# Banded attention on one core: TensorE's order fixed by hand, a tile's scores made beside the preceding tile

## The chip, the core and the metric

The kernel runs on one core of a Trainium2 chip. The metric is the device time of one execution in microseconds (us), lower is better. The engines are TensorE (PE in the rows, its weight loads PEld), VectorE (DVE), ScalarE (ACT), GpSimd (POOL, not used here) and SyncE (SP, which issues the DMAs). Each takes its instructions in the order in which they stand in its own list, and waits for the others by semaphores.

## What is computed

Two blocks of a model, each with two layers. The change lies in the attention of the second block's last layer: 256 tokens and 256 context tokens, 16 query heads that share 4 key and value heads of 64 channels, a window of 128 positions to both sides, and a sink, one more logit for each head that takes a share of the softmax and gives no value. Cut to what matters:

```python
s_ctx = einsum('bqhgd,bkhd->bhgqk', qb, kc)
s_win = where(allowed, einsum('bqhgd,bkhd->bhgqk', qb, kb), -inf)
p = softmax(concat([sink, s_ctx, s_win], -1), -1)[..., 1:]
o = einsum('bhgqk,bkhd->bqhgd', p[..., :ctx_len], vc) + einsum('bhgqk,bkhd->bqhgd', p[..., ctx_len:], vb)
x = x + gate * (o @ w_out)
```

Here only the tokens' outputs are needed, since the layer is the last.

## The kernel before, in words

The kernel is written with Python loops that are unrolled, and a scheduler orders each engine's instructions by priority (the place in the program) and by when it takes their inputs to be ready. Activations lie as channels by positions. `swa` (L1362) projects keys, values and queries, norms and rotates them, and then handles the 16 heads in eight tiles of two heads, `attend(t, ...)` (L1311). The output projection `residual` follows.

A tile t has two blocks of 128 queries (b) and two heads (f). For a block and a head:
- scores `swa_s`: two products of 512 columns, the keys' high and low part against queries of which the two halves of the partitions hold high and low part (L1326), and the band's mask, added by a product with the identity (L1327);
- the row maximum on VectorE (L1328), for both heads then the negative scaled maximum `swa_nm` (L1330) and the sink's logit `swa_es` (L1331);
- the exponential `swa_p` on ScalarE with its sum in `swa_z` (L1334);
- four transposes to `swa_pt` (L1337), copied to `swa_ps` by ScalarE for head 0 (L1341) and by VectorE for head 1 (L1339).

Then for the whole tile the row scale: the sinks' exponentials (L1342), the sum (L1343), its reciprocal (L1344), spread to 128 columns in `swa_zw` (L1346), two transposes into a `swa_pt` bank (L1349) and a copy to `swa_zs` (L1351). The 16 value products `swa_o` (L1357; the trace shows 32, two for each) are multiplied by `swa_zs` (L1360) and split into high and low part `xh`, `xl` for the projection (L139, L140).

Four PSUM banks hold scores (shared with the projections), two hold transposes, one the value products, and one is the chain's own for all other names:

```python
with ch.psum_pool("swas", {"pj": (4, "proj proj2 v swa_s"), "hn": (2, "hn_ss hn_bc swap swa_pt"), "o": (1, "swa_o")}):
```

The second group of queries is normed in `head_group`: sums of squares `hn_ss` (L1255), a chain of small steps on VectorE for the scale, its transposes `hn_bc` (L1264), the rotation product `swap` (L1269) with `swa_u` and `swa_rot` on VectorE, twice. The scheduler was free to lay scores of tiles 0 and 1 between these, and parts of a tile between those of another.

Of the kernel before, what the change touches and what calls it, by code (L numbers as in the profile page):

```python
# [13 lines left out]
AF = mybir.ActivationFunctionType  # L14
ALU = mybir.AluOpType
AX = mybir.AxisListType
PSUM = bass.MemoryType.PSUM

P = 128
D = 1024  # L20
KD = D // P
S = 256
# [80 lines left out]
class Kernel:  # L103
# [1204 lines left out]
            self.mm3(ps, [((x[0][:, k, b // 2, t], x[1][:, k, b // 2, t]), (ws[k // 4][0][:, k % 4], ws[k // 4][1][:, k % 4])) for k in range(KD)])  # L1308
            nc.scalar.activation(out[:, b], ps, AF.Copy)

    def attend(self, t, qs, ks, vs, sink, nsink, y):  # L1311

        nc, ch = self.nc, self.ch
        V, G = nc.vector, nc.scalar
        g = t // 4
        z, nm, es = (ch.loc([P, 2, 2], n, bufs=2) for n in ("swa_z", "swa_nm", "swa_es"))
        ps = ch.loc([P, 2, 4, 2, P], "swa_ps", bufs=2)
        for b in range(2):
            q, own = slice(b * P, (b + 1) * P), slice((1 - b) * P, (2 - b) * P)
            m = ch.loc([P, 2], "swa_m", bufs=3)  # L1320
            ss = []
            for f in range(2):
                s = ch.psum([P, 2, S], "swa_s")
                flat = s.rearrange("p j t -> p (j t)")
                for i, k in enumerate(ks):
                    nc.tensor.matmul(flat, qs[:, f, t, q], k[:, f, g].rearrange("p j t -> p (j t)"), start=i == 0, stop=False)  # L1326
                nc.tensor.matmul(s[:, 1, own], self.identb, self.tri[:, 1 - b], start=False, stop=True)  # L1327
                V.tensor_reduce(m[:, f:f + 1], s, AX.XY, ALU.max)  # L1328
                ss.append(s)
            V.scalar_tensor_tensor(nm[:, b], m, -0.125, nsink, op0=ALU.mult, op1=ALU.min)  # L1330
            V.tensor_tensor(es[:, b], nm[:, b], sink, op=ALU.add)  # L1331
            for f, s in enumerate(ss):
                p = ch.loc([P, 2, S], "swa_p", bufs=4)
                G.activation(p, s, AF.Exp, bias=nm[:, b, f:f + 1], scale=0.125, accum_out=z[:, b, f:f + 1])  # L1334
                pt = ch.psum([P, 4, P], "swa_pt")
                for k in range(4):
                    nc.tensor.transpose(pt[:, k], p[:, k // 2, (k % 2) * P:(k % 2 + 1) * P], self.ident)  # L1337
                if f:
                    V.tensor_copy(ps[:, f, :, b], pt)  # L1339
                else:  # L1340
                    G.activation(ps[:, f, :, b], pt, AF.Copy)  # L1341
        G.activation(es, es, AF.Exp)  # L1342
        V.tensor_tensor(z, z, es, op=ALU.add)  # L1343
        V.reciprocal(z, z)  # L1344
        zw = ch.loc([P, 2, P], "swa_zw", bufs=2)
        G.activation(zw.rearrange("p b (f d) -> p (b f) d", f=2), z.rearrange("p b f -> p (b f)").unsqueeze(2).to_broadcast((P, 4, 64)), AF.Copy)  # L1346
        zb = ch.psum([P, 2, P], "swa_pt")
        for b in range(2):
            nc.tensor.transpose(zb[:, b], zw[:, b], self.ident)  # L1349
        zs = ch.loc([P, S], "swa_zs", bufs=2)  # L1350
        G.activation(zs, zb.rearrange("p b t -> p (b t)"), AF.Copy)  # L1351
        o = ch.psum([P, S], "swa_o")
        for b in range(2):
            for k in range(4):
                for f in range(2):
                    v = vs[:, k, 64 * (2 * g + f):64 * (2 * g + f) + 64]
                    nc.tensor.matmul(o[64 * f:64 * f + 64, b * P:(b + 1) * P], v, ps[:, f, k, b], start=k == 0, stop=k == 3,  # L1357
                                     tile_position=(0, 64 * f))
        on = ch.loc([P, S], "swa_on", bufs=2)
        V.tensor_tensor(on, o, zs, op=ALU.mult)  # L1360
        self.split(on, y[0][:, t], y[1][:, t])

    def swa(self, h, x, gate):

        nc, ch, A = self.nc, self.ch, self.A
        V, G = nc.vector, nc.scalar
        with ch.phase("swa"):
            with ch.psum_pool("swas", {"pj": (4, "proj proj2 v swa_s"), "hn": (2, "hn_ss hn_bc swap swa_pt"), "o": (1, "swa_o")}):
                self.swa_tables = [self.load_const(n, F32, ch.ph) for n in ("swa_cos", "swa_sin")]
                qs = ch.loc([P, 2, 8, S], "swa_q", F32R)  # L1370
                ks = [ch.loc([P, 2, 2, 2, S], n, F32R) for n in ("swa_kh", "swa_kl")]
                vs = ch.loc([P, 4, S], "swa_v")
                one = [t[:, :, 1] for t in x]
                keys = self.project_apart([(A["swa_w"], 8 + i) for i in range(2)], x, lambda: self.kv_values(x, vs, (0, 1)))
                self.head_group([keys[i][:, j] for j in range(2) for i in range(2)], self.col("swa_k_gain"), (False, True),
                                lambda i, t: self.stack_keys(ks, i // 2, t))
                for g in range(2):
                    self.head_group([lambda i=i: self.project(A["swa_w"], 4 * g + i, one) for i in range(4)], self.col("swa_q_gain"),
                                    (True, True), lambda i, t: self.stack_queries(qs, 4 * g + i, t))
                    if g == 0:  # L1380
                        self.kv_values(x, vs, (2, 3))
                y = self.own
                sink = self.col("swa_sink")
                nsink = ch.loc([P, 16], "swa_nsink")
                V.tensor_scalar(nsink, sink, -1.0, None, op0=ALU.mult)
                for t in range(8):
                    self.attend(t, qs, ks, vs, sink[:, 2 * t:2 * t + 2], nsink[:, 2 * t:2 * t + 2], y)
                return self.residual(h, A["swa_out"], y, gate)


# [259 lines left out]
```

## Time and profile before

| | us |
|---|---|
| median of 3 runs (lowest, highest) | 3152.95 (3150.81, 3155.64) |
| the profiled execution, its own time | 3151.34 |
| its span in the trace | 3149.4 |
| TensorE, matmuls busy (weight loads) | 3093.1 (2689.0) |
| VectorE, ScalarE busy | 2284.7, 1747.3 |
| mean granted clock of TensorE, as a share of full speed | 0.993 |

Times within the span count from its start. A timeline row is: start, duration, engine, line, operation, output<-inputs, shapes, count of merged instructions, and in square brackets the idle time of the engine just before, with what ended it. Matmuls overlap in TensorE's pipeline, so a row's duration is longer than the step to the next row; the step is what a matmul costs in a dense stretch.

### The profile page before, as it was taken

What the parts mean: (1) busy time and instruction counts of PE and PEld (TensorE: products, weight loads), DVE (VectorE), ACT (ScalarE), POOL (GpSimd) and SP (SyncE); (2) the same over time, 40 slices, a digit from 0 to 9 for tenths busy, and PEclk for the clock granted to TensorE, in tenths of its full rate; (3) what the DMA queues carried; (4) which work ended last, traced back from release to release, by engine and by line L of the source; (5) the groups of instructions that cost most, each with busy time, mean ns of one, the idle gap of its engine ahead of it and who ended that gap; (6) DMA issues with size and microseconds to landing.
All of it is one profiled execution on the core that took longest, in us unless ns stands there. A gap on an engine that the chain in (4) does not pass through costs nothing.

```text
span 3149.4 us, 54554 instructions
## 1 busy us (share of the span) xinstructions
PE 3093.1 (98%) x20526; PEld 2689.0 (85%) x20526; DVE 2284.7 (73%) x4912; ACT 1747.3 (55%) x3553; POOL 0.2 (0%) x4
## 2 busy tenths in 40 slices
PE   8999999999999989999999999999999999998999
PEld 8978999999889988888777778888888888895899
DVE  7767776877777786566788888767776766676666
ACT  5546555655565554444576767545554455565554
POOL 0000000000000000000000000000000000000000
PEclk9999999999999999999999999999999999999999
DMA  7563556666445544443311111245553444440465
GB/s 243 182 211 127 168 177 212 206 186 191 162 160 182 182 134 128 131 140 122 91 41 35 34 48 35 94 135 165 162 170 111 144 139 141 140 137 21 128 182 166
DMA packets 129720, 437.91 MB, mean 139 GB/s; under 512 B 14513, under 2 KB 18225, under 8 KB 129073
## 3 DMA queue, kind: packets, MB, share of 16 engines
q1 hardware_dynamic: 129456, 434.43, 43.7%
q8 instruction: 161, 2.64, 0.3%
q14 instruction: 103, 0.84, 0.1%
HBM read 432.28 MB, written 1.05 MB: 138 GB/s over the span
## 4 chain that ended last, share of the span: by engine, by line
PE 91%; DVE 4%; ACT 2%; DMA 1%; issue 1%; SPq 0%; ACTq 0%; DVEq 0%
PE gu L165 15%; PE gu L166 15%; PE gu L167 14%; PE dn L165 7%; PE dn L166 7%; PE dn L167 6%; PE proj L166 4%; PE proj L165 4%; PE proj L167 4%; PE ada L476 1%; DVE wlo L140 1%; PE dn_pw L995 1%; PE swa_o L1357 1%; PE dn_px L995 1%; PE ms L220 1%
## 5 line engine op out<-in xcount | busy, mean ns | idle before, releaser
L139 ACT ACTIVATE whi<-raw 128x512 fp32r<-128x512 f32 (+1 forms) x1398 | 841.1, 605 | 1026.0 <-PE gu L166 513.0
L140 DVE TENSOR_TENSOR wlo<-raw,whi 128x512 fp32r<-128x512 f32 (+1 forms) x1398 | 913.6, 658 | 543.0 <-ACT whi L139 524.4
L165 PE MATMUL gu<-xh,whi 128*128 128x256 f32 (+1 forms) x2800 | 907.0, 324 | 11.7 <-ACT xh L306 8.8
L166 PE MATMUL gu<-xl,whi 128*128 128x256 f32 (+1 forms) x2800 | 906.5, 324 | 0.2 <-DVE xl L307 0.2
L167 PE MATMUL gu<-xh,wlo 128*128 128x256 f32 (+1 forms) x2800 | 905.2, 324 | 0.1
L165 PEld LDWEIGHTS gu<-xh,whi 128*128 128x128 f32 x2800 | 529.7, 189 | 63.2 <-ACT xh L306 10.7
L166 PEld LDWEIGHTS gu<-xl,whi 128*128 128x128 f32 x2800 | 529.6, 189 | 52.3 <-issue 5.4
L167 PEld LDWEIGHTS gu<-xh,wlo 128*128 128x128 f32 x2800 | 529.1, 189 | 49.7 <-issue 3.7
L165 PE MATMUL dn<-hh,whi 128*128 128x256 f32 (+1 forms) x1388 | 444.9, 322 | 1.3
L166 PE MATMUL dn<-hl,whi 128*128 128x256 f32 (+1 forms) x1388 | 444.3, 321 | 0.0
L167 PE MATMUL dn<-hh,wlo 128*128 128x256 f32 (+1 forms) x1388 | 443.1, 320 | 0.0
L165 PE MATMUL proj<-xh,whi 128*128 128x256 f32 (+2 forms) x936 | 306.0, 330 | 4.9 <-ACT lora_raw L550 1.9
L166 PE MATMUL proj<-xl,whi 128*128 128x256 f32 (+2 forms) x936 | 307.5, 329 | 2.0 <-DVE xl L299 1.6
L167 PE MATMUL proj<-xh,wlo 128*128 128x256 f32 (+2 forms) x936 | 306.8, 329 | 1.6 <-DVE wlo L140 1.6
L165 PEld LDWEIGHTS dn<-hh,whi 128*128 128x128 f32 x1388 | 260.5, 188 | 27.3 <-ACT hh L139 5.5
L166 PEld LDWEIGHTS dn<-hl,whi 128*128 128x128 f32 x1388 | 260.8, 188 | 24.2 <-DVE hl L140 2.8
L167 PEld LDWEIGHTS dn<-hh,wlo 128*128 128x128 f32 x1388 | 260.3, 188 | 21.1
L436 DVE TENSOR_TENSOR ada_t<-ada_w,ada_c 128x1024 f32<-128x1024 f32 x192 | 226.3, 1219 | 0.0
L437 ACT ACTIVATE ada_t<-ada_t 128x1024 f32<-128x1024 f32 x192 | 201.2, 1050 | 29.9 <-DVE ada_t L436 29.5
L165 PEld LDWEIGHTS proj<-xh,whi 128*128 128x128 f32 (+1 forms) x936 | 176.0, 189 | 16.6 <-issue 5.5
L166 PEld LDWEIGHTS proj<-xl,whi 128*128 128x128 f32 (+1 forms) x936 | 176.8, 189 | 15.0 <-DVE xl L299 4.5
L167 PEld LDWEIGHTS proj<-xh,wlo 128*128 128x128 f32 (+1 forms) x936 | 176.7, 189 | 11.4 <-issue 2.4
(521 smaller groups left out, 3769.6 us busy)
## 6 DMA issues: line engine op xcount, KB each, us to landing
raw<-in_ffn_gate SPq DMA_DIRECT2D x176, 512.0 KB, 3.6
raw<-in_ffn_up SPq DMA_DIRECT2D x176, 512.0 KB, 3.6
ada_w<-in_ada_w SPq DMA_DIRECT2D x96, 512.0 KB, 3.6
raw<-in_ffn_down SPq DMA_DIRECT2D x80, 448.0 KB, 3.4
adaw<-in_ada_w SPq DMA_DIRECT2D x48, 512.0 KB, 4.9
raw<-in_ffn_down SPq DMA_DIRECT2D x40, 512.0 KB, 3.5
raw<-in_ffn_down SPq DMA_DIRECT2D x48, 384.0 KB, 3.2
raw<-in_dn_w SPq DMA_DIRECT2D x32, 512.0 KB, 3.5
```

Of the source, the lines that this page charges most:

```text
L139: self.nc.scalar.activation(hi, src, AF.Copy)
L140: return self.nc.vector.tensor_tensor(lo, src, hi.bitcast(F32), op=ALU.subtract)
L165: self.nc.tensor.matmul(out, ah, bh, start=first and i == 0, stop=False)
L166: self.nc.tensor.matmul(out, ah, bl, start=False, stop=False)
L167: self.nc.tensor.matmul(out, al, bh, start=False, stop=last and i == n - 1)
L220: self.nc.tensor.matmul(ms[:, i, b:b + 1], acc[:, j, b * P:(b + 1) * P], self.ones[:, :1], start=j == 0, stop=j == 1)
L436: V.tensor_tensor(p, w, c[:, s], op=ALU.mult)
L437: G.activation(p, p, AF.Copy, accum_out=sums[:, j, k, s:s + 1])
L476: nc.tensor.matmul(ps[32 * i:32 * i + 32], self.cond[:, k], raw[:, i], start=k == 0, stop=k == KD - 1, tile_position=(0, 32 * i))
L995: nc.tensor.matmul(out[:, c], lhs[:, c], rhs[:, c], start=more is None, stop=True, skip_group_check=more is not None)
L1357: nc.tensor.matmul(o[64 * f:64 * f + 64, b * P:(b + 1) * P], v, ps[:, f, k, b], start=k == 0, stop=k == 3, tile_position=(0, 64 * f))
```

## The change

`attend` now holds the loop over the tiles, and two helpers the parts of a tile: `scores` (scores, maximum, exponentials of one block) and `turn` (transposes and copies of one block). In the loop a tile's first transposes are followed by the next tile's scores of block 0, then its second transposes, the transposes of the row scale, the next tile's scores of block 1, and its value products. Every matmul of these is `pinned`: the scheduler has to place it behind whatever TensorE instruction was written before it. The other engines' instructions, and TensorE's other ones, are ordered by the scheduler as before. `swa_p` has six buffers instead of four, the small tiles three instead of two, and the row scale's transposes `swa_zb` fall to the chain's own bank.

```diff
--- before.py
+++ after.py
@@ -1308,57 +1308,93 @@
             self.mm3(ps, [((x[0][:, k, b // 2, t], x[1][:, k, b // 2, t]), (ws[k // 4][0][:, k % 4], ws[k // 4][1][:, k % 4])) for k in range(KD)])
             nc.scalar.activation(out[:, b], ps, AF.Copy)
-    def attend(self, t, qs, ks, vs, sink, nsink, y):
+    def pinned(self, ins):
+        return self.tc.keep_in_program_order(ins)
+    def scores(self, t, b, qs, ks, sink, nsink, st):
         nc, ch = self.nc, self.ch
         V, G = nc.vector, nc.scalar
         g = t // 4
+        q, own = slice(b * P, (b + 1) * P), slice((1 - b) * P, (2 - b) * P)
+        m = ch.loc([P, 2], "swa_m", bufs=3)
+        ss = []
+        for f in range(2):
+            s = ch.psum([P, 2, S], "swa_s")
+            flat = s.rearrange("p j t -> p (j t)")
+            for i, k in enumerate(ks):
+                self.pinned(nc.tensor.matmul(flat, qs[:, f, t, q], k[:, f, g].rearrange("p j t -> p (j t)"), start=i == 0, stop=False))
+            ss.append(s)
+        for f, s in enumerate(ss):
+            self.pinned(nc.tensor.matmul(s[:, 1, own], self.identb, self.tri[:, 1 - b], start=False, stop=True))
+            V.tensor_reduce(m[:, f:f + 1], s, AX.XY, ALU.max)
+        V.scalar_tensor_tensor(st["nm"][:, b], m, -0.125, nsink, op0=ALU.mult, op1=ALU.min)
+        V.tensor_tensor(st["es"][:, b], st["nm"][:, b], sink, op=ALU.add)
+        for f, s in enumerate(ss):
+            p = ch.loc([P, 2, S], "swa_p", bufs=6)
+            G.activation(p, s, AF.Exp, bias=st["nm"][:, b, f:f + 1], scale=0.125, accum_out=st["z"][:, b, f:f + 1])
+            st["p"].append(p)
+    def turn(self, b, st):
+        nc, ch = self.nc, self.ch
+        for f in range(2):
+            p = st["p"][2 * b + f]
+            pt = ch.psum([P, 4, P], "swa_pt")
+            for k in range(4):
+                self.pinned(nc.tensor.transpose(pt[:, k], p[:, k // 2, (k % 2) * P:(k % 2 + 1) * P], self.ident))
+            if f:
+                nc.vector.tensor_copy(st["ps"][:, f, :, b], pt)
+            else:
+                nc.scalar.activation(st["ps"][:, f, :, b], pt, AF.Copy)
+    def attend(self, qs, ks, vs, sink, nsink, y):
+        nc, ch = self.nc, self.ch
+        V, G = nc.vector, nc.scalar
+        def scores(t, b, st):
+            if t < 8:
+                self.scores(t, b, qs, ks, sink[:, 2 * t:2 * t + 2], nsink[:, 2 * t:2 * t + 2], st)
+        def state(t):
+            st = {n: ch.loc([P, 2, 2], "swa_" + n, bufs=3) for n in ("z", "nm", "es")}
+            return st | {"p": [], "ps": ch.loc([P, 2, 4, 2, P], "swa_ps", bufs=2)}
+        st = state(0)
         for b in range(2):
+            scores(0, b, st)
+        for t in range(8):
+            g = t // 4
+            after = state(t + 1) if t < 7 else None
+            z, es = st["z"], st["es"]
+            self.turn(0, st)
+            scores(t + 1, 0, after)
+            G.activation(es, es, AF.Exp)
+            V.tensor_tensor(z, z, es, op=ALU.add)
+            V.reciprocal(z, z)
+            zw = ch.loc([P, 2, P], "swa_zw", bufs=2)
+            G.activation(zw.rearrange("p b (f d) -> p (b f) d", f=2), z.rearrange("p b f -> p (b f)").unsqueeze(2).to_broadcast((P, 4, 64)), AF.Copy)
+            self.turn(1, st)
+            zb = ch.psum([P, 2, P], "swa_zb")
+            for b in range(2):
+                self.pinned(nc.tensor.transpose(zb[:, b], zw[:, b], self.ident))
+            zs = ch.loc([P, S], "swa_zs", bufs=2)
+            G.activation(zs, zb.rearrange("p b t -> p (b t)"), AF.Copy)
+            scores(t + 1, 1, after)
+            o = ch.psum([P, S], "swa_o")
+            for b in range(2):
                 for k in range(4):
+                    for f in range(2):
+                        v = vs[:, k, 64 * (2 * g + f):64 * (2 * g + f) + 64]
+                        self.pinned(nc.tensor.matmul(o[64 * f:64 * f + 64, b * P:(b + 1) * P], v, st["ps"][:, f, k, b], start=k == 0, stop=k == 3,
+                                                     tile_position=(0, 64 * f)))
+            on = ch.loc([P, S], "swa_on", bufs=2)
+            V.tensor_tensor(on, o, zs, op=ALU.mult)
+            self.split(on, y[0][:, t], y[1][:, t])
+            st = after
     def swa(self, h, x, gate):
@@ -1383,8 +1419,7 @@
                 sink = self.col("swa_sink")
                 nsink = ch.loc([P, 16], "swa_nsink")
                 V.tensor_scalar(nsink, sink, -1.0, None, op0=ALU.mult)
-                for t in range(8):
-                    self.attend(t, qs, ks, vs, sink[:, 2 * t:2 * t + 2], nsink[:, 2 * t:2 * t + 2], y)
+                self.attend(qs, ks, vs, sink, nsink, y)
                 return self.residual(h, A["swa_out"], y, gate)
```

TensorE, tile 6 of the kernel before, from its first transposes on, with scores (`swa_s`) of tile 7 in between; the row scale is the transpose of `swa_zw`:

```order
L1337 MATMUL swa_pt<-ident,swa_p 128x128 x4
L1326 MATMUL swa_s<-swa_kh,swa_q 128x512
L1337 MATMUL swa_pt<-ident,swa_p 128x128 x4
L1357 MATMUL swa_o<-swa_ps,swa_v 64x128
L1326 MATMUL swa_s<-swa_kl,swa_q 128x512
L1327 LDWEIGHTS identb
...
L1337 MATMUL swa_pt<-ident,swa_p 128x128 x4
L1357 MATMUL swa_o<-swa_ps,swa_v 64x128 x3
L1349 MATMUL swa_pt<-ident,swa_zw 128x128 x2
L1357 MATMUL swa_o<-swa_ps,swa_v 64x128 x10
L1326 MATMUL swa_s<-swa_kl,swa_q 128x512
```

The same place now, tiles 1 to 6:

```order
L1346 MATMUL swa_pt<-ident,swa_p 128x128 x8
L1327 MATMUL swa_s<-swa_kh,swa_q 128x512
L1327 MATMUL swa_s<-swa_kl,swa_q 128x512
...
L1330 MATMUL swa_s<-tri,identb 128x128
L1346 MATMUL swa_pt<-ident,swa_p 128x128 x8
L1383 MATMUL swa_zb<-ident,swa_zw 128x128 x2
L1327 MATMUL swa_s<-swa_kh,swa_q 128x512
...
L1330 MATMUL swa_s<-tri,identb 128x128
L1392 MATMUL swa_o<-swa_ps,swa_v 64x128 x16
```

The value products, in four pieces before, are one piece at the end, and the transposes of the row scale now stand ahead of the second block's scores and of all value products.

ScalarE, one tile of the kernel before (tiles 2 to 6), from its first exponentials to its row scale and its split:

```order
L1334 ACTIVATE swa_p,swa_z<-swa_s,swa_nm 128x512 x2
L1341 ACTIVATE swa_ps<-swa_pt 128x4x128
L1334 ACTIVATE swa_p,swa_z<-swa_s,swa_nm 128x512 x2
L1342 ACTIVATE swa_es<-swa_es 128x4
L1341 ACTIVATE swa_ps<-swa_pt 128x4x128
L1346 ACTIVATE swa_zw<-swa_z 128x256
L1351 ACTIVATE swa_zs<-swa_pt 128x256
L139 ACTIVATE xh<-swa_on 128x256
```

ScalarE now, tiles 1 to 6; the exponentials are the next tile's:

```order
L1350 ACTIVATE swa_ps<-swa_pt 128x4x128
L1375 ACTIVATE swa_es<-swa_es 128x4
L1350 ACTIVATE swa_ps<-swa_pt 128x4x128
L1336 ACTIVATE swa_p,swa_z<-swa_s,swa_nm 128x512 x2
L1379 ACTIVATE swa_zw<-swa_z 128x256
L1385 ACTIVATE swa_zs<-swa_zb 128x256
L1336 ACTIVATE swa_p,swa_z<-swa_s,swa_nm 128x512 x2
L139 ACTIVATE xh<-swa_on 128x256
```

The row scale `swa_zw` of a tile stood ahead of all exponentials of the next; it now stands behind those of the next tile's first block. In tile 0 alone it is still ahead of them.

VectorE now, tiles 1 to 6:

```order
L1348 COPY swa_ps<-swa_pt 128x4x128
L140 TENSOR_TENSOR xl<-swa_on,xh 128x256
L1331 TENSOR_REDUCE swa_m<-swa_s 128x1 x2
L1376 TENSOR_TENSOR swa_z<-swa_z,swa_es 128x4
L1348 COPY swa_ps<-swa_pt 128x4x128
L1332 SCALAR_TENSOR_TENSOR swa_nm<-swa_m,swa_nsink 128x2
L1377 RECIPROCAL swa_z<-swa_z 128x4
L1333 TENSOR_TENSOR swa_es<-swa_nm,small 128x2
```

The maximum `swa_nm` of the next tile's first block, and behind it this tile's reciprocal, stand behind the copy of this tile's second transposes.

## Rows read from the trace of the kernel before

**Rows 1.** The page, part 4: shares of the chain that ended last, by engine.
```profile
PE 91%; DVE 4%; ACT 2%; DMA 1%; issue 1%; SPq 0%; ACTq 0%; DVEq 0%
```

**Rows 2.** Busy time by stretch: stretch, length, busy us of PE, PEld, DVE, ACT, POOL; clock; DMA; GB/s.
```profile
2880.00:2890.00 10.00, 9.17 (x76) 6.08 (x76) 6.12 (x15) 5.53 (x16) 0.00 (x0) 1.00 0.00 0
```

**Rows 3.** Timeline of TensorE, first instruction of tiles 0, 1, 2, 7 and behind: start us, us.
```profile
2859.47 0.66 PE L1337 MATMUL swa_pt<-ident,swa_p 128*128 128x128 f32 x4 [1.70 <-DVE swa_u L1272]
...
2868.84 1.09 PE L1337 MATMUL swa_pt<-ident,swa_p 128*128 128x128 f32 x8
...
2876.40 0.66 PE L1337 MATMUL swa_pt<-ident,swa_p 128*128 128x128 f32 x4 [0.81 <-ACT swa_p L1334]
...
2919.68 0.65 PE L1337 MATMUL swa_pt<-ident,swa_p 128*128 128x128 f32 x4 [0.82 <-ACT swa_p L1334]
...
2925.64 0.39 PE L165 MATMUL proj<-xh,whi 128*128 128x256 f32 x1
```

**Rows 4.** Timeline of TensorE in tile 1, which it ran without a break.
```profile
2869.77 0.22 PE L1327 MATMUL swa_s<-tri,identb 128*128 128x128 bf16 x1
...
2871.62 0.38 PE L1349 MATMUL swa_pt<-ident,swa_zw 128*128 128x128 f32 x2
2871.93 1.96 PE L1357 MATMUL swa_o<-swa_ps,swa_v 128*64 128x128 f32 x30
2873.82 0.50 PE L1326 MATMUL swa_s<-swa_kl,swa_q 128*128 128x512 f32 x1
...
2874.21 0.48 PE L1326 MATMUL swa_s<-swa_kh,swa_q 128*128 128x512 f32 x1
...
2875.36 0.23 PE L1327 MATMUL swa_s<-tri,identb 128*128 128x128 bf16 x1
```

**Rows 5.** Timeline of VectorE in tile 6 and at the start of tile 7's scores.
```profile
2910.06 0.69 DVE L1328 TENSOR_REDUCE swa_m<-swa_s 128x1 f32<-128x512 f32 x1
...
2910.73 0.69 DVE L1328 TENSOR_REDUCE swa_m<-swa_s 128x1 f32<-128x512 f32 x1
2911.45 0.16 DVE L1330 SCALAR_TENSOR_TENSOR swa_nm<-swa_m,swa_nsink 128x2 f32<-128x2 f32 x1
...
2912.38 0.69 DVE L1339 COPY swa_ps<-swa_pt 128x512 f32<-128x512 f32 x1 [0.57 <-PE swa_pt L1337]
2913.34 0.69 DVE L1328 TENSOR_REDUCE swa_m<-swa_s 128x1 f32<-128x512 f32 x1 [0.26 <-PE swa_s L1327]
2913.95 0.15 DVE L1343 TENSOR_TENSOR swa_z<-swa_z,swa_es 128x4 f32<-128x4 f32 x1
```

**Rows 6.** Timeline of ScalarE in tile 6.
```profile
2910.18 0.69 ACT L1334 ACTIVATE swa_p<-swa_s,swa_nm 128x512 f32<-128x512 f32 x1 [0.67 <-DVE swa_nm L1330]
...
2910.86 0.68 ACT L1334 ACTIVATE swa_p<-swa_s,swa_nm 128x512 f32<-128x512 f32 x1
...
2914.56 0.41 ACT L1346 ACTIVATE swa_zw<-swa_z 128x256 f32<-128x256 f32 x1
```

**Rows 7.** Timeline of TensorE: three lulls, in square brackets, with what ended them.
```profile
231.00 0.38 PE L165 MATMUL proj<-xh,whi 128*128 128x256 f32 x1 [1.91 <-ACT lora_raw L550]
...
275.59 0.61 PE L683 MATMUL g_t<-ident,g_rows 64*128 64x64 f32 x2 [1.50 <-DVE g_rows L671]
...
2848.97 0.50 PE L1326 MATMUL swa_s<-swa_kh,swa_q 128*128 128x512 f32 x1 [2.75 <-ACT swa_p L1334]
```

**Rows 8.** Busy time by stretch, columns as in rows 2: stretches behind lulls, then tiles 2 to 6.
```profile
232.00:236.00 4.00, 4.00 (x24) 4.00 (x22) 1.24 (x6) 1.01 (x2) 0.00 (x0) 0.57 0.95 352
276.00:280.00 4.00, 3.98 (x14) 2.61 (x15) 3.22 (x8) 1.90 (x6) 0.00 (x0) 0.57 0.34 99
2850.00:2854.00 4.00, 4.00 (x13) 2.25 (x12) 2.24 (x6) 1.96 (x6) 0.00 (x0) 0.57 0.02 4
2860.00:2868.00 8.00, 7.31 (x40) 4.95 (x40) 3.58 (x6) 5.09 (x12) 0.00 (x0) 0.57 0.00 0
2876.00:2920.00 44.00, 39.45 (x313) 26.53 (x314) 27.87 (x73) 26.63 (x73) 0.00 (x0) 1.00 0.01 1
```

More of the change, by code (lines that the diff above doesn't have):

```diff
@@ L1315, in attend @@
         g = t // 4
-        z, nm, es = (ch.loc([P, 2, 2], n, bufs=2) for n in ("swa_z", "swa_nm", "swa_es"))
-        ps = ch.loc([P, 2, 4, 2, P], "swa_ps", bufs=2)
-        for b in range(2):
[L1319 to L1335, printed above, removed]
-                for k in range(4):
[L1337 to L1361, printed above, removed]
+        q, own = slice(b * P, (b + 1) * P), slice((1 - b) * P, (2 - b) * P)
```

## Prediction, made before the changed kernel ran

> **What bounds the kernel now.** I read the chain that ended last first: TensorE holds 91% of it [rows 1], so a change to TensorE's order counts where TensorE waits. Next, the busy time by stretch: in 10 us of the banded attention TensorE shows 9.17 us busy, its weight loads 6.08, VectorE 6.12, ScalarE 5.53, DMA nothing, clock 1.00 [rows 2]. So the stage is about 66 us of 3150, and no engine is full in it. Then the timeline, to cut it into tiles at the first transpose of each: tile 0 begins at 2859.47, tile 1 at 2868.84, tile 2 at 2876.40, tile 7 at 2919.68, and its last value products hand over to the output projection at 2925.64 [rows 3]. Tiles 2 to 6 take (2919.68 - 2876.40) / 5 = 8.66 us each; tile 1 takes 7.56, tile 0 9.37. Each tile begins with a lull of about 0.82 us, for the exponential [rows 3].
>
> **What TensorE needs in a tile.** From tile 1, which ran without a break [rows 3, 4]: 8 transposes, a block's share, in 0.93 us (2868.84 to 2869.77), so 0.94 for a block with a little for the step between groups and 1.88 for a tile; the two row-scale transposes 0.31 (2871.62 to 2871.93); 30 value products 1.89 (to 2873.82), so 2.0 for 32, and 2.2 with the handover between 64- and 128-column tiles. Two sets of scores, with their masks, take 2874.21 to 2875.36 plus the last mask: 1.2; with the masks together I take 1.15 for a block, 2.3 for a tile. Sum 6.7 us, against 8.66 now: this is what a better order could win.
>
> **The change, part by part.**
> Instructions and their forms stay the same in number; no DMA is added or moved, and the stage moves next to no data [rows 2]. The larger rings (six exponentials, three of the small tiles, a bank of its own for the row scale) only take waits away, and I cost them at nothing: the waits that decide below are for data.
>
> What decides is where ScalarE puts the row scale `swa_zw` (L1379 of the change). In tiles 1 to 6 it stands behind the two exponentials of the next tile's first block; these wait for the row maximum `swa_nm`, which on VectorE stands behind two reductions and the second transposes' copy. TensorE's fixed order puts the row-scale transposes ahead of the second block's scores and the 32 value products, so all of these wait for `swa_zw`. Before, they did not: `swa_zw` came before the next tile's exponentials, and TensorE had value products on both sides of its transposes. From the end of the first block's scores to the row-scale transposes, link by link:
> - two reductions: 0.69 each, 0.60 to 0.67 apart [rows 5]: 1.3;
> - the sum `swa_z` (0.07 of VectorE's time, my estimate from how closely its small steps follow in rows 5) and the copy, 0.69 [rows 5]: 0.75;
> - the maximum: 0.16 [rows 5], and 0.04 to ScalarE: 0.2;
> - two exponentials, 2910.18 to 2911.54 [rows 6]: 1.36;
> - `swa_zw`, 0.41 [rows 6], and 0.05 to TensorE: 0.46.
> Together 4.05 us. Of this TensorE fills 0.94 with the second block's transposes, so it stands still for 3.1 us. From there it runs: row-scale transposes 0.3, scores 1.15, values 2.2, first transposes of the next tile 0.94, their scores 1.15: 5.75. A tile takes 4.05 + 5.75 = 9.8 us. Six such tiles take 58.8; tiles 1 to 6 took 2919.68 - 2868.84 = 50.84. **Plus 8.0 us.** If my links are 0.2 wrong, this is 1.2 either way.
>
> Then the clock. After lulls of 1.91, 1.50 and 2.75 us [rows 7] the granted clock fell from 1.00 to 0.50, that is from 2.4 to 1.2 GHz, with means of 0.57 over the 4 us that hold each fall [rows 8]. There are nine falls between 200 and 3140 us (the first two, the seventh and the eighth stand in rows 8), and each lull of 1.5 us or more is followed by one; the lulls of 0.82 of tiles 2 to 6 left it at 1.00 [rows 8]. Six of the nine cost (1 - 0.57) x 4 = 1.7 us of full-speed work each, three cost twice that, in the row from 2860 8 us at a mean of 0.57 [rows 8]. A lull of 3.1 us in each of six tiles, with 6 us of dense work behind it that is all on the path, should therefore cost one short fall per tile: 6 x 1.7 = **plus 10.2 us.** The bounds are nothing (no fall) and 6 x 3.4 = 20.4. I take the short fall, since the long ones in rows 8 had further lulls inside, and here work follows without a break. The Trainium skill ("TensorE: Matmul & The Clock Gate", HAM oscillation) describes the same price, paid anew in each pass of a loop with a wait in it, but only for waits longer than the 3.1 us here; by its rule there would be no fall, and the sum would be +7.6 (rival 2). The rows speak against it: 1.50 us was enough [rows 7].
>
> The start. The first pinned score comes behind the last rotation product (`swap`) of the queries, while before the scores of tiles 0 and 1 filled gaps of the second query group. Cover lost: a block's scores, two reductions, the maximum and the exponentials of tile 0 now come behind the queries, 1.15 + 1.3 + 0.2 + 1.36 = 4.0 us. Gained: up to eight reductions leave VectorE's chain for the queries, 8 x 0.60 = 4.8 [rows 5]; the first transpose at 2859.47 waited for that chain (`swa_u`), not for its own data [rows 3]. So -0.8 if all is gained, +2.4 if a third is; I take +0.8, the middle. Tile 0 keeps a good order (its row scale stands ahead of the exponentials): 6.7 of work and about 1 of waits, 7.7 us at full clock or 9.4 with one fall, against 9.37; I take -0.8. The end: in tile 7, 5.96 us long now [rows 3], there are no next scores, and eight projection products instead of six fit in; I take -0.4, between -1 and 0.
>
> **Sum:** 8.0 + 10.2 + 0.8 - 0.8 - 0.4 = +17.8 us. The profiled execution took 3151.34 us for a span of 3149.4, so it would become 3169.1; it lies 1.6 below the median of the runs, 3152.95, from which I get 3170.8, rounded to **3171**. Less than 0.2%, 6.3 us, can't be told from no change here.
>
> **Rivals.**
> 1. Faster: ScalarE gets the row scale out in time. If `swa_zw` were done within the 0.94 us of the second transposes, TensorE would never stand still and a tile would cost its 6.7 us of work: 6 x (8.47 - 6.7) = 10.6 less, 3142 us. For it: tile 0 has that order, and weight loads of 6.08 in 10 us leave room [rows 2]. The Trainium skill ("Perfetto Trace Analysis", Identifying the Most-Contended Engine) holds that matmul busy time is no good measure of how near TensorE is to its limit, and the weight loads' share a better one; by that the room is there, and the 6.7 of 8.66 us from rows 4 agree. Against it: the printed order of ScalarE in tiles 1 to 6. The point that decides is whether the row scale stands ahead of the exponentials.
> 2. The lulls come, the clock holds: 8.0 - 0.4 = +7.6, 3160.5 us. For it: the lulls are regular, and with long dense work between them. Against: each of [rows 7].
> 3. The falls are long ones, or come with a second lull: +28, 3181 us. For it: three of nine were so, among them this very stage at 2860 [rows 8].
> 4. Nothing to see: the links overlap more than I let them (for instance the first reduction starts under the second block's mask), the start gains its 0.8 us and no lull tips the clock: within 6 us.
>
> **How the numbers follow.** My forecast 0.60, rival 1 0.04, rival 2 0.18, rival 3 0.12, rival 4 0.06. The range takes in rival 2 with its 1.2 and the start's bounds, down to 3157, and rival 3 up to 3184; it leaves out rival 1, most of rival 4 and the worst of rival 3, under 0.2. Slower by over 0.2%: the forecast, rival 3 and nearly all of rival 2, 0.88. Faster: rival 1, 0.04. The rest is 0.08.
>
> **What would show it.** In the profile of the changed kernel: the row-scale transposes at L1383 with an idle of some 3 us before them, six times, released by ScalarE's `swa_zw` at L1379 (right), or none (rival 1). ScalarE's second pair of exponentials waiting about 2 us for `swa_nm`. First transposes 11 to 12 us apart (9.8 in rival 2, 13 in rival 3). Granted clock of 0.50 once in each tile for 3 to 4 us behind the lull. The first score at about 2853 and the first transpose near 2860. The forecast is wrong at its root if tiles 1 to 6 take 8.7 us or less, or if the lull ends at something other than `swa_zw`.

## The result and the profile after

The changed kernel took 3169.62 us (median of 6 runs, 3167.57 to 3174.66), the kernel before 3151.99 (6 runs, 3149.70 to 3155.64). The ratio is 1.0057, with a 95% interval of 1.0044 to 1.0069: slower. Beside two later experiments it was run again, 3165.67 against 3152.57, a ratio of 1.0041 (1.0029 to 1.0053). The profiled execution took 3169.32 us for a span of 3167.4.

The shares of the chain that ended last hardly moved against [rows 1]:

```profile
PE 92%; DVE 4%; ACT 2%; DMA 1%; issue 1%; SPq 0%; ACTq 0%; DVEq 0%
```

They can't show it: 18 us of 3150 are half a per cent. The stage must be cut out. Busy time by stretch of the changed kernel (PE, PEld, DVE, ACT and POOL busy, then the granted clock): the ten us that answer to [rows 2], then tiles 1 to 6, from the first transposes of tile 1 to those of tile 7, then two falls of the clock in them.

```profile
2880.00:2890.00 10.00, 7.31 (x60) 5.76 (x58) 5.26 (x14) 4.79 (x14) 0.00 (x0) 0.83 0.01 2
2873.36:2939.66 66.30, 48.52 (x375) 38.52 (x373) 31.54 (x84) 31.29 (x87) 0.00 (x0) 0.82 0.00 1
2880.00:2884.00 4.00, 4.00 (x36) 3.23 (x36) 1.61 (x4) 1.41 (x4) 0.00 (x0) 0.57 0.00 0
2910.90:2917.60 6.70, 5.82 (x39) 4.91 (x40) 1.61 (x4) 2.66 (x8) 0.00 (x0) 0.50 0.00 0
```

TensorE, busy 9.17 of 10 us before, is busy 7.31. Tiles 1 to 6 take 66.30 us, 11.05 each, where they took 50.84 [rows 3], and their mean clock is 0.82 where it was 1.00. There are six falls in them, one beginning within 0.9 us of each lull's end: five short ones like the row from 2880 and one of twice the length (2910.9 to 2917.6).

The waits of TensorE and of ScalarE in tiles 1 to 6 (engine, tile and line, released by what; us in total, times, longest):

```profile
PE swa_zb L1383 <- ACT swa_zw L1379: 17.8, 6, 3.0
...
ACT swa_p L1336 <- DVE swa_nm L1332: 23.8, 13, 3.0
```

TensorE waits for one thing only, the row scale, six times 2.96 us. One of these waits in the timeline: TensorE in tile 1 and at the start of tile 2, then VectorE and ScalarE in the same tile (start, duration, what, and in square brackets the idle time before it and what ended it).

```profile
2873.36 1.09 PE L1346 MATMUL swa_pt<-ident,swa_p 128*128 128x128 f32 x8
...
2875.34 1.05 PE L1346 MATMUL swa_pt<-ident,swa_p 128*128 128x128 f32 x8
2879.35 0.44 PE L1383 MATMUL swa_zb<-ident,swa_zw 128*128 128x128 f32 x2 [2.96 <-ACT swa_zw L1379]
...
2881.22 3.12 PE L1392 MATMUL swa_o<-swa_ps,swa_v 128*64 128x128 f32 x32
```

```profile
2875.49 1.29 DVE L1331 TENSOR_REDUCE swa_m<-swa_s 128x1 f32<-128x512 f32 x2
2876.69 0.15 DVE L1376 TENSOR_TENSOR swa_z<-swa_z,swa_es 128x4 f32<-128x4 f32 x1
2876.76 0.68 DVE L1348 COPY swa_ps<-swa_pt 128x512 f32<-128x512 f32 x1
2877.36 0.15 DVE L1332 SCALAR_TENSOR_TENSOR swa_nm<-swa_m,swa_nsink 128x2 f32<-128x2 f32 x1
2877.43 0.17 DVE L1377 RECIPROCAL swa_z<-swa_z 128x4 f32<-128x4 f32 x1
```

```profile
2877.55 0.69 ACT L1336 ACTIVATE swa_p<-swa_s,swa_nm 128x512 f32<-128x512 f32 x1 [0.96 <-DVE swa_nm L1332]
...
2878.23 0.68 ACT L1336 ACTIVATE swa_p<-swa_s,swa_nm 128x512 f32<-128x512 f32 x1
...
2878.89 0.41 ACT L1379 ACTIVATE swa_zw<-swa_z 128x256 f32<-128x256 f32 x1
...
2882.80 0.69 ACT L1336 ACTIVATE swa_p<-swa_s,swa_nm 128x512 f32<-128x512 f32 x1 [2.59 <-DVE swa_nm L1332]
```

This is the chain of the prediction, link behind link: two reductions, the sum and the copy, the maximum, two exponentials, and only then `swa_zw`, although the reciprocal that it spreads was ready at 2877.60, 1.3 us before. From 2875.49 to 2879.35 it takes 3.86 us; TensorE has 0.9 us of transposes in it and then stands still for 2.96. Behind the lull the clock falls, and the 32 value products, 1.97 us at full clock (a row of the next run), take 3.12.

The start, answering to the first row of [rows 3] and the third of [rows 7]:

```profile
2853.01 1.12 PE L1264 MATMUL hn_bc<-ident,hn_wide 128*128 128x128 f32 x4 [3.50 <-ACT hn_wide L1259]
...
2865.39 0.66 PE L1346 MATMUL swa_pt<-ident,swa_p 128*128 128x128 f32 x4 [4.03 <-ACT swa_p L1336]
```

Before, the scores of tile 0 were made early, with a lull of 2.75 us ahead of them [rows 7]; now there is a lull of 3.50 us for the queries and one of 4.03 us for the first exponentials.

In this execution the work upstream of the stage, the same in both programs, already ran 4.5 us late (2848.89 against 2844.35 at the last sum of squares of the queries), through falls of the clock that come at other places in each execution; such drift is part of the spread of the runs. So the experiments below are read by tiles 1 to 6 first, and by the ratio second.

### The profile page after: what moved, and what is told of

Read it like the earlier page. It is cut to its first block, busy times and chain, and to the rows that moved or that the text cites. A ratio compares the mean times of both kernels' runs of the same rounds, so it can differ in the third digit from the quotient of the medians.

```text
span 3167.4 us, 54544 instructions
## 1 busy us (share of the span) xinstructions
PE 3093.7 (98%) x20526; PEld 2695.9 (85%) x20526; DVE 2282.6 (72%) x4912; ACT 1746.0 (55%) x3553; POOL 0.2 (0%) x4
## 4 chain that ended last, share of the span: by engine, by line
PE 92%; DVE 4%; ACT 2%; DMA 1%; issue 1%; SPq 0%; ACTq 0%; DVEq 0%
PE gu L165 14%; PE gu L166 14%; PE gu L167 14%; PE dn L165 7%; PE dn L166 7%; PE dn L167 7%; PE proj L166 4%; PE proj L165 4%; PE proj L167 4%; PE ada L476 1%; DVE wlo L140 1%; PE dn_pw L995 1%; PE dn_px L995 1%; PE swa_o L1392 1%; PE dn_pt L995 1%
```

## The experiments

Theory: (a) TensorE waits because ScalarE does `swa_zw` behind the next tile's exponentials while the fixed order has TensorE wait for it; (b) the lull and the clock are two costs, about 8 and 10 us in the prediction's sum. Rivals: any fixed order costs this; the restructured program does; the falls have another cause. Each run was compared with the kernel before, run beside it.

### The row scale first

```diff
-            self.turn(0, st)
-            scores(t + 1, 0, after)
             G.activation(es, es, AF.Exp)
             V.tensor_tensor(z, z, es, op=ALU.add)
             V.reciprocal(z, z)
...
+            self.turn(0, st)
+            scores(t + 1, 0, after)
             self.turn(1, st)
```

> The four small steps of the row scale (the sink's exponential, the sum, the reciprocal, swa_zw) stand ahead of the first transposes and of the next tile's first scores, so that ScalarE does swa_zw before the next tile's exponentials; TensorE's fixed order is the changed kernel's. Theory (the place of swa_zw on ScalarE makes the lull, and the lull makes the clock fall): swa_zw now waits only for the second transposes' copy, 0.47 + 0.69 + 0.41 us against 0.94 us of transposes, so a lull of at most 0.9 us is left; no fall of the clock in tiles 1 to 6; tiles of 6.8 to 7.8 us instead of 11.05, so 20 to 26 us under the changed kernel and 4 to 10 us under the kernel before, a ratio of 0.997 to 0.999. Rival A (any order fixed by hand costs this, wherever the row scale stands): still 10 us or more a tile, within 5 us of the changed kernel. Rival B (the lull goes, but the clock falls for another reason): tiles of 8.5 to 9.5 us, 0 to +5 us against before.

3141.53 us, a ratio of 0.9965 (0.9954 to 0.9977). Tiles 1 to 6 by stretch, two rows of TensorE and two of ScalarE in tile 2:

```profile
2879.19:2920.65 41.46, 38.13 (x374) 30.70 (x373) 31.32 (x84) 29.76 (x85) 0.00 (x0) 1.00 0.01 1
```
```profile
2889.68 0.44 PE L1383 MATMUL swa_zb<-ident,swa_zw 128*128 128x128 f32 x2 [0.55 <-ACT swa_zw L1377]
...
2891.10 1.97 PE L1392 MATMUL swa_o<-swa_ps,swa_v 128*64 128x128 f32 x32
```
```profile
2889.22 0.41 ACT L1377 ACTIVATE swa_zw<-swa_z 128x256 f32<-128x256 f32 x1
...
2890.44 0.68 ACT L1336 ACTIVATE swa_p<-swa_s,swa_nm 128x512 f32<-128x512 f32 x1
```

TensorE's order is the changed kernel's, word for word; ScalarE now does `swa_zw` ahead of the next tile's exponentials. The lull is 0.55 us, the clock 1.00, a tile 6.91 us. That refutes rival A, and shows (a): the loss hangs on whether the row scale's four small steps, `swa_zw` last of them, stand ahead of the next tile's exponentials. The gain is a little larger than the forecast, 0.997 to 0.999.

### The lull filled

```diff
             zb = ch.psum([P, 2, P], "swa_zb")
+            for i in range(22 if 0 < t < 7 else 0):
+                self.pinned(nc.tensor.transpose(zb[:, i % 2], self.ident, self.ident))
```

> The changed kernel with 22 transposes of the identity added in each of tiles 1 to 6 where TensorE stands still for swa_zw, 22 x 0.117 = 2.6 us at full clock; they write into the row scale's bank, which its own two transposes then overwrite. The wait itself stays, TensorE is busy in it. Theory (lull and clock are two costs, and the clock falls because TensorE stands still): no fall in tiles 1 to 6; tiles of 9.3 to 9.8 us; 8 to 11 us under the changed kernel, 6 to 10 us above the kernel before, a ratio of 1.002 to 1.003. Rival A (the falls come from somewhere else, or cost nothing because the path runs on ScalarE and VectorE): tiles stay at 11 us, within 3 us of the changed kernel. Rival B (the filler delays the row scale's transposes): tiles over 11 us, slower than the changed kernel.

3157.11 us, a ratio of 1.0011 (1.0000 to 1.0021). Tiles 1 to 6, and one of the six waits that are left, behind the filler:

```profile
2866.30:2922.24 55.94, 52.55 (x507) 45.13 (x505) 31.56 (x84) 30.44 (x85) 0.00 (x0) 1.00 0.00 1
```
```profile
2869.18 2.56 PE L1383 MATMUL swa_zb<-ident 128*128 128x128 f32 x22
2872.31 0.44 PE L1385 MATMUL swa_zb<-ident,swa_zw 128*128 128x128 f32 x2 [0.57 <-ACT swa_zw L1379]
```

From the second transposes to the row scale's it is 4.01 us (2868.30 to 2872.31), as in the changed kernel (2875.34 to 2879.35): the wait is untouched. Only the clock is, 1.00 where it was 0.82. 132 transposes that nobody needs made the stage 66.30 - 55.94 = 10.36 us faster. So the two costs part: the stall is 55.94 - 50.84 = 5.10 us, the clock 10.36. The ratio came out under the 1.002 to 1.003 of the forecast, since the stall is smaller than the 8 us of the prediction's sum.

### The lull half filled

As above, with `range(11 if ...)`.

> As the filler run, but with 11 added transposes instead of 22: 1.3 us of the 2.96 us are filled, a lull of about 1.9 us is left in each of tiles 1 to 6, and the row scale's transposes start no earlier or later. Theory (a lull of this length is answered by a fall of the clock, as the one of 1.91 us early in the profile of before was; what the filler saved was the clock and not the wait): the falls are back in tiles 1 to 6, tiles of about 11 us, within 4 us of the changed kernel, a ratio of 1.004 to 1.007. Rival A (only the full lull of 3 us matters to the clock): no falls in tiles 1 to 6, tiles of 9.3 us, and the ratio of the full filler, 1.000 to 1.002. Rival B: falls in some tiles, and a time between the two.

3157.25 us, a ratio of 1.0017 (1.0009 to 1.0026).

```profile
2872.89:2928.83 55.94, 45.35 (x440) 37.93 (x439) 31.57 (x84) 30.39 (x85) 0.00 (x0) 1.00 0.00 1
```
```profile
PE swa_zb L1385 <- ACT swa_zw L1379: 10.6, 6, 1.8
```

My theory missed here, and rival A was right: six lulls of 1.77 us, and no fall. The tiles take 55.94 us to the hundredth, as with the full filler, which bears out the split into 5.10 and 10.36. But it takes away a reason that the prediction gave for the clock's term, as told below.

### The row-scale transposes last

```diff
-            zb = ch.psum([P, 2, P], "swa_zb")
-            for b in range(2):
-                self.pinned(nc.tensor.transpose(zb[:, b], zw[:, b], self.ident))
-            zs = ch.loc([P, S], "swa_zs", bufs=2)
-            G.activation(zs, zb.rearrange("p b t -> p (b t)"), AF.Copy)
             scores(t + 1, 1, after)
             o = ch.psum([P, S], "swa_o")
...
+            zb = ch.psum([P, 2, P], "swa_zb")
+            for b in range(2):
+                self.pinned(nc.tensor.transpose(zb[:, b], zw[:, b], self.ident))
+            zs = ch.loc([P, S], "swa_zs", bufs=2)
+            G.activation(zs, zb.rearrange("p b t -> p (b t)"), AF.Copy)
             on = ch.loc([P, S], "swa_on", bufs=2)
```

> Only the place of the two row-scale transposes in TensorE's fixed order changes: behind the value products instead of ahead of the second block's scores. Theory (TensorE loses the time because its queue waits at these transposes with ready work behind them): swa_zw may come 3 us later without anybody waiting, so no lull over 1 us and no fall in tiles 1 to 6; tiles of 6.8 to 7.8 us; 20 to 26 us under the changed kernel, 4 to 10 us under the kernel before, a ratio of 0.997 to 0.999. Rival A (the chain of reductions, maximum and exponentials bounds a tile whatever stands where): a wait of 2 to 3 us turns up at another place, the first transposes of a tile, and tiles stay over 9.5 us.

3141.36 us, a ratio of 0.9960 (0.9946 to 0.9974).

```profile
2878.32:2917.73 39.41, 37.69 (x379) 31.34 (x377) 30.10 (x84) 29.85 (x85) 0.00 (x0) 1.00 0.00 1
```
```profile
PE swa_zb L1391 <- ACT swa_zw L1379: 1.7, 5, 0.4
```

Here `swa_zw` is still behind the exponentials of the next tile's first block, but TensorE asks for it 3 us later, with the second block's scores and the 32 value products done in between. A tile takes 6.57 us, less than the 6.8 to 7.8 of the forecast. Either end of the wait can be moved: earlier on ScalarE or later on TensorE. What costs is a fixed place ahead of ready work.

### Without the fixed order

```diff
     def pinned(self, ins):
 
-        return self.tc.keep_in_program_order(ins)
+        return ins
```

> The changed kernel's program, but TensorE's instructions aren't held to the program's order: the scheduler places them, as before, and puts the row-scale transposes of a tile behind its value products. Theory (only where the fixed order puts the row-scale transposes matters): no lull over 1.5 us in tiles 1 to 6, tiles of 7 to 8.5 us, and the first scores fill gaps of the queries again, so the start's 1 to 2 us come back; 16 to 26 us under the changed kernel, between 9 us under and 2 us above the kernel before. Rival (the restructured program, its larger rings and the row scale's own bank, costs the time): over 9.5 us a tile, within 6 us of the changed kernel.

3137.07 us, a ratio of 0.9950 (0.9937 to 0.9963). From the row-scale transposes of tile 1 to those of tile 7 TensorE has no idle time, 38.05 us or 6.3 a tile; below it, two rows of tile 5:

```profile
2870.35:2908.40 38.05, 38.05 (x391) 32.21 (x389) 30.32 (x82) 29.64 (x83) 0.00 (x0) 1.00 0.01 2
```
```profile
2891.81 0.44 PE L1346 MATMUL swa_pt<-ident,swa_p 128*128 128x128 f32 x2
2892.08 0.38 PE L1383 MATMUL swa_zb<-ident,swa_zw 128*128 128x128 f32 x2
```

In tiles 3 to 6 the scheduler puts the row scale's transposes between the next tile's first ones, where by then nobody has to wait for `swa_zw`. A tile was forecast at 7 to 8.5 us, too long. The restructured program without the fixed order is faster than before by 0.5%, so the restructuring doesn't cost the time. Which part of it wins (the order of the program, the larger rings, the bank of its own) was not tried.

### The start, and the best order

Three runs on one chip, the changed kernel again among them, and later a fourth. In one, only the scores of tile 0 were left out of the fixed order; in another, moreover, the row-scale transposes stand behind the next tile's first transposes; the fourth run has this second edit alone.

```diff
-    def pinned(self, ins):
+    def pinned(self, ins, t=1):
 
+        if t == 0:
+            return ins
         return self.tc.keep_in_program_order(ins)
...
-                self.pinned(nc.tensor.matmul(flat, qs[:, f, t, q], k[:, f, g].rearrange("p j t -> p (j t)"), start=i == 0, stop=False))
+                self.pinned(nc.tensor.matmul(flat, qs[:, f, t, q], k[:, f, g].rearrange("p j t -> p (j t)"), start=i == 0, stop=False), t)
...
-            self.pinned(nc.tensor.matmul(s[:, 1, own], self.identb, self.tri[:, 1 - b], start=False, stop=True))
+            self.pinned(nc.tensor.matmul(s[:, 1, own], self.identb, self.tri[:, 1 - b], start=False, stop=True), t)
```
```diff
+        self.turn(0, st)
         for t in range(8):
...
-            self.turn(0, st)
             scores(t + 1, 0, after)
...
-            zb = ch.psum([P, 2, P], "swa_zb")
-            for b in range(2):
-                self.pinned(nc.tensor.transpose(zb[:, b], zw[:, b], self.ident))
-            zs = ch.loc([P, S], "swa_zs", bufs=2)
-            G.activation(zs, zb.rearrange("p b t -> p (b t)"), AF.Copy)
             scores(t + 1, 1, after)
...
+            st = after
+            if t < 7:
+                self.turn(0, st)
+            zb = ch.psum([P, 2, P], "swa_zb")
+            for b in range(2):
+                self.pinned(nc.tensor.transpose(zb[:, b], zw[:, b], self.ident))
+            zs = ch.loc([P, S], "swa_zs", bufs=2)
+            G.activation(zs, zb.rearrange("p b t -> p (b t)"), AF.Copy)
             on = ch.loc([P, S], "swa_on", bufs=2)
```

> The changed kernel with the scores of tile 0 alone not held to the program's order; tiles 1 to 7 as they were. Theory of the prediction (the pinned start loses 4.0 us of cover and gains about 3 us on VectorE's chain for the queries): the 4.0 us lull ahead of the first transposes goes, the queries end later, and 0 to 3 us are won over the changed kernel; tiles 1 to 6 stay at 11 us. Rival A (the whole cover of 4.0 us and a fall of the clock are lost by the pinned start): 4 to 7 us won. Rival B (VectorE's chain decides): nothing won, or up to 2 us lost.

> The changed kernel as it is, beside the two others on the same chip: 1.004 to 1.007 of the kernel before, by every theory; it shows how far the runs of one kernel differ from one set to the next.

> Fixed order again, with two edits: the row-scale transposes of a tile behind the first transposes of the next tile, so that swa_zw has 0.9 us more than where they stood behind the value products (there 0.34 us of wait was left in each tile), and the scores of tile 0 not held to the program's order, so that the scheduler can put them among the queries again. Theory (TensorE's work alone is left, 6.2 us a tile, and the start comes back as in the kernel without fixed order): tiles of 6.1 to 6.4 us, no lull over 0.5 us in tiles 1 to 6, no lull of 3 to 4 us ahead of the first transposes; 3132 to 3139 us, a ratio of 0.9935 to 0.996, level with the kernel without fixed order or up to 5 us under it. Rival (a fixed order is worse than the scheduler's even with the waits out of it): above that kernel by 2 us or more.

> The run with both edits, without the freed scores of tile 0: fixed order throughout, the row-scale transposes behind the next tile's first transposes. Theory (the start is worth nothing either way, and the 0.34 us of wait that the place behind the value products left is gone): tiles of 6.2 us against 6.55 there, so 3137 to 3141 us, within 3 us of the run with both edits. Rival (the freed scores of tile 0 harm, because the clock stayed at half for 17 us at the start of that run): 3 to 6 us faster than it, 3132 to 3135 us.

Ratios: tile 0's scores free 1.0035 (1.0023 to 1.0047), the changed kernel beside it 1.0041 (1.0029 to 1.0053), both edits 0.9949 (0.9938 to 0.9961), the second edit alone 0.9968 (0.9955 to 0.9981). By stretch: tiles 1 to 6 of the changed kernel again; the start of the run with tile 0's scores free; tiles 1 to 6 with the second edit alone.

```profile
2873.84:2941.66 67.82, 50.01 (x375) 39.73 (x373) 31.58 (x84) 32.02 (x88) 0.00 (x0) 0.80 0.00 1
```
```profile
2848.60:2865.90 17.30, 12.95 (x40) 8.13 (x40) 10.48 (x22) 7.75 (x18) 0.00 (x0) 0.52 0.01 1
```
```profile
2870.79:2907.95 37.16, 37.16 (x374) 30.74 (x372) 29.75 (x82) 29.25 (x84) 0.00 (x0) 1.00 0.01 2
```

The freed start wins nothing that can be told: the two ratios' intervals overlap almost wholly. From the last of the queries' sums of squares to the first transposes of tile 1 it takes 24.07 us (2844.13 to 2868.20) against 24.45 (2849.39 to 2873.84): the lull of 4.0 us goes, but the one ahead of the queries' `hn_bc` grows from 3.50 to 4.38 us (below), and in this execution the clock stays at half for 17 us, where there were two short falls.

```profile
2850.36 0.90 PE L1264 MATMUL hn_bc<-ident,hn_wide 128*128 128x128 f32 x3 [4.38 <-ACT hn_wide L1259]
```

The second edit leaves TensorE without a pause in tiles 1 to 6: 37.16 us, 6.19 a tile (37.32 in the run with both edits, 6.22), as forecast in both. That is the work alone. With both edits the time is level with the scheduler's order, as forecast; with the second alone it is 3140.47 us, within the forecast's 3137 to 3141, so its rival, that the freed start harms, falls. But against the run with the transposes last, its gain of 0.38 us a tile, 2.2 us in all, doesn't show in the ratios (0.9968 and 0.9960): that is below what these runs can tell.

## Why the prediction was right, and where its sizes were off

The time was: 3171 predicted, 3169.62 measured, well inside the range. By steps, in the profiled execution:

- **The mechanism: right.** The row-scale transposes wait for `swa_zw` six times, 2.96 us where 3.1 was predicted; ScalarE's second exponentials wait for `swa_nm`, 2.59 us in tile 1 (about 2 predicted); first transposes 11.05 us apart (11 to 12 predicted).
- **The stall: +5.1 us instead of +8.0.** This is the term most mis-sized. With the lull filled, a tile is 9.32 us and not 9.8. From the first transposes to the second it takes 2.00 us (2866.30 to 2868.30), 2.09 predicted; from the second to the row scale's 4.01 (4.05 predicted, though the links listed there add up to 4.07); from there to the next tile's first transposes 3.32 (2872.31 to 2875.63), and here the prediction had 3.65. Its parts: row-scale transposes 0.19 us (0.3 predicted), a block's scores 1.23 (1.15), the 32 value products 1.90 (2.2, of which 0.2 for a handover between tiles of 64 and 128 columns that no run shows). Six times 0.48 are the 2.9 us.
- **The clock: +10.4 instead of +10.2**, from 66.30 - 55.94, which is closer than its reasons deserve: by the prediction's own prices, five short falls and a long one would have been 11.9; in the second profile of the changed kernel, with two long falls instead of one, 67.82 - 55.94 = 11.9. But the reason was wrong in part: the prediction held that each lull of 1.5 us or more is followed by a fall, from [rows 7, 8]. Six lulls of 1.77 us were not. The lulls here were nearly 3 us, so the term stood. The Trainium skill ("TensorE: Matmul & The Clock Gate", HAM oscillation) warns only of idle gaps longer than any of these six; by its rule there would have been no fall. The trace disagrees: the six lulls of 2.96 us each brought one, and so did one of 2.32 us in the run with tile 0's scores free.
- **The start and tile 0: 0 together, as predicted**, with larger parts: 24.47 us from the last sum of squares of the queries to tile 1 (2848.89 to 2873.36), 24.49 before (2844.35 to 2868.84). Tile 0 itself takes 7.97 us instead of 9.37 (-1.4, predicted -0.8), although a fall lies in it, for which the prediction had 9.4; the start took the rest (+1.4, predicted +0.8). Freeing tile 0's scores won no more than 0.4 us of it.
- **The end: -0.7** (tile 7 takes 5.26 us, 2939.66 to 2944.92, for 5.96), -0.4 predicted.

The stage is thus 5.1 + 10.4 + 0 - 0.7 = 14.8 us longer where the prediction had 17.8. The medians say 17.6 in one set of runs and 13.1 in the other; that the forecast came within 1.4 us of the first is partly luck. The profiled execution is 18.0 us longer, but 4.5 of this arose upstream of the stage, and 1.3 were won back behind it. Of the rivals, the second (the clock holds) is what the filler made: 1.0011 and 1.0017, where it had foretold 7.6 us, 1.0024; the 5.1 - 0.7 = 4.4 us that the stall and the end leave are 1.0014. The first, a tile of 6.7 us, is what the edits of ScalarE's or TensorE's order made, 6.2 to 6.9 us (TensorE's work alone is 6.19, half a microsecond under the prediction's 6.7); its deciding point was named rightly, whether `swa_zw` stands ahead of the exponentials.

Not settled: what besides a lull's length decides on a fall. It isn't the place in the program: the eleven profiles have the same instructions up to the stage, and the same early lull goes either way in them. That of 1.50 to 1.52 us ahead of `g_t` (the second of [rows 7]) was followed by a fall in eight of them and by none in three; that ahead of `proj` (the first), where it was 1.81 to 2.08 us, by a fall in three of nine. So one trace of the kernel before couldn't give the rule, and six lulls of 1.77 us without a fall, seen in one profile, don't give its opposite. Here is the lull at `g_t` in the run with tile 0's scores free, with the clock behind it (0.57 in [rows 8]):

```profile
274.67 0.73 PE L683 MATMUL g_t<-ident,g_rows 64*128 64x64 f32 x4 [1.51 <-DVE g_rows L671]
```
```profile
275.00:279.00 4.00, 3.25 (x17) 2.14 (x17) 3.30 (x8) 2.57 (x8) 0.00 (x0) 1.00 0.31 98
```

How long the half clock lasts isn't settled either, but the 17 us at the start can't be put down to the freed scores. The run with the transposes last had over 20 us of it behind that same early lull (first row), far ahead of the change, and the run with the second edit alone, its start in the fixed order, had 17 us at its start in two pieces:

```profile
277.80:298.20 20.40, 20.40 (x71) 15.53 (x69) 6.16 (x22) 7.22 (x17) 0.00 (x0) 0.50 0.14 45
```
```profile
2847.20:2857.40 10.20, 7.43 (x16) 3.80 (x16) 4.58 (x9) 2.31 (x3) 0.00 (x0) 0.50 0.00 1
2860.90:2867.60 6.70, 5.21 (x22) 4.49 (x23) 4.78 (x11) 4.92 (x13) 0.00 (x0) 0.50 0.02 4
```

## What to carry to other kernels

Fixing one engine's order makes each of its waits a wait for everything behind it; so before a hand-made order is fixed, follow each operand that comes back from another engine, and see in which place that engine's own order makes it. Here one 0.41 us step behind two exponentials cost 15 us, and moving either end of that wait made the kernel faster than the one before by 0.3 to 0.5%. Price a stall of this length on TensorE twice, the wait and the clock after it; a filler run tells the two apart.

## What was not expected of the hardware

Throw-away work paid: 11 added transposes per tile (1.36 us of TensorE) won back as much as 22, 10.36 us in six tiles, because the granted clock stayed at 2.4 GHz. And the clock's answer to a lull is told only in part by its length: in the eleven profiles, the wait at the kernel's start aside, each of the 56 lulls of 2.19 us or more had a fall to 1.2 GHz in it or within 2.3 us of its end, those of 0.55 us and six of 1.77 had none, and lulls of 1.50 to 2.08 us went either way, the same lull in different executions of the same instructions. The time at half speed was 3 to 4 us mostly, near 7 or 10 at times, and 17 to 20 in four of the profiles.
